# Thirteen low weight parts by ScalarE and adding transfers, and one more FFN channel by shared sums

## The chip, the core and the metric

The kernel runs on one core of a Trainium2 chip. The metric is the device time of one execution in microseconds (us). The engines are TensorE (PE in the profile; PEld is its weight load), VectorE (DVE), ScalarE (ACT), GpSimd (POOL) and SyncE (SP); sixteen DMA engines move data. Transfers are issued on SyncE's queue, and those that add to what is in the on-chip memory (SBUF) on GpSimd's.

## What is computed

One layer of a decoder trunk for 512 tokens and 1024 channels in float32, with a convolution branch and a gated linear attention branch, an output projection, and a channel mixer (FFN) of inner width F = 2816. The change lies in the up part of the FFN:

```
u2 = _rmsnorm(h, norm2_g[l])
z = _causal_dwconv(u2 @ w_ffn_up[l], ffn_dw_w[l], ffn_dw_b[l])      # 2F columns, three taps
h = h + (jax.nn.silu(z[..., :FFN_DIM]) * z[..., FFN_DIM:]) @ w_ffn_down[l]
```

## The kernel before

**Products in three.** Every float32 weight tile (128 x 1024, 512 KB) is split into a high part `whi`, rounded to the format that TensorE multiplies fast, and a low part `wlo` = tile - high. Activations are split alike (`uh`, `ul`). A product is three: low weight x high activation, high x low, high x high (`mm3`, lines 529 to 531), in this order for each of eight slices k of 128 channels.

**Splitting.** `split_weight` works through the list `order` of all weight tiles. For a plain tile, ScalarE casts `raw` to `whi` (L444) and VectorE subtracts (L452). For tiles in the set `ADDED`, all in the layer's first part until now, ScalarE writes -raw, rounded, into `wlo` (L446), and a transfer from GpSimd's queue adds the tile from DRAM to it (L447). There are four buffers each for `raw`, `whi` and `wlo`. `weight` hands a tile to the products and has the two tiles after it split (`LOOK = 2`).

**The up part.** The 2816 inner channels are 22 "channels" of 128, and each needs two tiles of `w_up`: i for the value and 22 + i for the gate. A channel is done in one of two ways:
- plain: two tiles of 24 products of 512 columns, each into one PSUM bank (`col_tile`);
- by shared sums (`two_tiles`, a "unit"): both tiles together, with seven block products in place of eight. It has four parts: x1, x3 and x2 with 24 products of 256 columns each, x4 with 12. The weight sums are made by GpSimd (`two_sums`, L386), the four subtractions for them by VectorE (L415), and the token sums of the activations once before (`ffn_sums`). ScalarE copies finished products out of PSUM (`put`, L1338), VectorE combines others (L1341). In x1 it copies the first of two products while PE makes the second; x3 then adds into the same bank.

Channels come in pairs, in three groups (`GROUPS`). After a channel's products come the convolution taps (L1717, L1720), silu (L1728) and the gating (`first_gated`, `first_of_pair` for the first of a pair, `second_of_pair` for the second). After each group its down part (`seven`, steps of `w_down`) uses the pairs.

**Order.** `up_plan` writes out, for each group, the sequence of pieces of plain tiles, parts of units and gatings. PE works in that order. The instructions of the other engines are put in order by a scheduler that has a cost for each and follows the order of the program as priority; `tc.issue_after` adds an order by hand. Before, channels 0, 2, 1, 3 and 4 in group 0 and 19 in group 2 are plain and uncut, channels 6, 7, 10, 11, 21, 14, 15 and 18 are units, and each unit has a plain channel's tiles cut into pieces between its parts: piece, x1, piece, x3, and so on.

## Time and profile before

| | |
|---|---|
| median of three runs | 819.33 us (818.31, 819.33, 819.45) |
| the profiled execution | 818.28 us |
| its span, first to last instruction | 816.5 us |
| mean granted TensorE clock | 0.998 |
| moved by DMA | 113.60 MB, mean 139 GB/s |

In the lines below, a row of the timeline has start, duration (both us), engine, source line, operation, out<-in. A row of a group has its count, busy time, mean duration in ns, and the idle time of the engine before it with what ended it. TensorE's durations overlap, since products are pipelined; the distance between starts is what one costs.

### The profile page before, as it was taken

How to read it: one execution, taken by the hardware profiler on the slowest of the kernel's cores; microseconds unless marked ns; L12 is line 12 of the kernel's file. 1: busy time of each engine (PE TensorE's matmuls, PEld its weight loads, DVE VectorE, ACT ScalarE, POOL GpSimd, SP SyncE). 2: the span in 40 equal slices, each digit the busy share in tenths (PEclk: the TensorE clock that was granted, in tenths of full speed). 3: DMA queues.
4: the chain of work that ended last, by engine and by line, in shares of the span. 5: the costliest groups of instructions: out<-in, count | busy, mean ns of one | idle time of the engine just before them, and what ended most of it. 6: DMA issues, size and time to landing. Idle time of an engine off the chain costs nothing.

```text
span 816.5 us, 11462 instructions
## 1 busy us (share of the span) xinstructions
PE 808.3 (99%) x4227; PEld 695.4 (85%) x4227; DVE 698.6 (86%) x1099; ACT 487.4 (60%) x744; POOL 197.9 (24%) x176
## 2 busy tenths in 40 slices
PE   9999999999999999999999999999999999999996
PEld 8888888788888898989888898898889988899885
DVE  6779999998998888486779899979966999789895
ACT  6667788677546575494435655556445663466554
POOL 2025434332204332122001100320123311621012
PEclk9999999999999999999999999999999999999999
DMA  8487858645831232432558513145732446335662
GB/s 329 148 195 178 196 160 179 158 114 133 192 90 65 78 130 78 136 108 93 163 132 217 184 60 123 52 154 156 147 131 83 142 117 167 104 104 180 156 129 104
DMA packets 36472, 113.60 MB, mean 139 GB/s; under 512 B 3688, under 2 KB 8944, under 8 KB 36416
## 3 DMA queue, kind: packets, MB, share of 16 engines
q1 hardware_dynamic: 28912, 86.39, 30.8%
q0 software_dynamic: 7488, 26.48, 18.7%
q8 instruction: 33, 0.54, 0.3%
q14 instruction: 23, 0.19, 0.1%
q10 hardware_dynamic: 16, 0.00, 0.0%
HBM read 110.76 MB, written 2.10 MB: 138 GB/s over the span
## 4 chain that ended last, share of the span: by engine, by line
PE 88%; DVE 11%; issue 0%; ACT 0%; POOL 0%; POOLq 0%; ACTq 0%; DVEq 0%
PE mm L529 20%; PE mm L530 20%; PE mm L531 20%; DVE c L889 5%; PE cv L529 4%; PE cv L530 4%; PE cv L531 4%; DVE aside L889 3%; PE ax L530 2%; PE ax L531 2%; PE ax L529 2%; PE mm L743 2%; PE ax L1217 1%; PE cv L743 1%; PE ax L1219 1%; PE mm L649 1%
## 5 line engine op out<-in xcount | busy, mean ns | idle before, releaser
L529 PE MATMUL mm<-uh,wlo 128*128 128x512 f32 (+1 forms) x532 | 193.9, 364 | 0.0
L530 PE MATMUL mm<-ul,whi 128*128 128x512 f32 (+1 forms) x532 | 191.5, 360 | 0.0
L531 PE MATMUL mm<-uh,whi 128*128 128x512 f32 (+1 forms) x532 | 191.4, 360 | 0.0
L415 DVE TENSOR_TENSOR wlo<-raw,whi 128x1024 fp32r<-128x1024 f32 x82 | 95.2, 1167 | 35.7 <-ACT whi L414 31.8
L386 POOL TENSOR_TENSOR raw<-raw,raw 128x512 f32<-128x512 f32 x39 | 62.7, 1609 | 234.3 <-DVE wlo L415 132.1
L529 PEld LDWEIGHTS mm<-uh,wlo 128*128 128x128 f32 x532 | 100.5, 189 | 15.3 <-DVE wlo L452 0.3
L531 PEld LDWEIGHTS mm<-uh,whi 128*128 128x128 f32 x532 | 100.4, 189 | 15.4
L530 PEld LDWEIGHTS mm<-ul,whi 128*128 128x128 f32 x532 | 100.5, 189 | 14.7
L414 ACT CAST whi<-raw 128x1024 fp32r<-128x1024 f32 x82 | 78.9, 966 | 39.3 <-PE mm L531 24.6
L444 ACT CAST whi<-raw 128x1024 fp32r<-128x1024 f32 x80 | 83.5, 1048 | 29.6 <-PE mm L531 13.9
L452 DVE TENSOR_TENSOR wlo<-raw,whi 128x1024 fp32r<-128x1024 f32 x50 | 66.2, 1329 | 7.2 <-ACT whi L444 7.0
L414 ACT CAST whi<-kept 128x1024 fp32r<-128x1024 f32 (+1 forms) x40 | 40.2, 1008 | 30.9 <-DVE kept L362 16.0
L415 DVE TENSOR_TENSOR wlo<-kept,whi 128x1024 fp32r<-128x1024 f32 (+1 forms) x40 | 47.5, 1187 | 5.8 <-ACT whi L414 5.8
L889 DVE SCALAR_TENSOR_TENSOR aside<-cv,pp,aside 128x255 f32<-128x255 f32 (+6 forms) x112 | 52.3, 467 | 0.0
L889 DVE SCALAR_TENSOR_TENSOR c<-aside,btmp,c 128x247 f32<-128x247 f32 (+13 forms) x93 | 52.2, 566 | 0.0
L889 DVE SCALAR_TENSOR_TENSOR c<-cv,pp,c 128x247 f32<-128x247 f32 (+13 forms) x93 | 43.3, 466 | 1.4 <-ACT c L885 1.4
L446 ACT ACTIVATE wlo<-raw 128x1024 fp32r<-128x1024 f32 x28 | 29.4, 1060 | 19.1 <-PE mm L529 19.1
L1338 ACT COPY tmp<-mm 128x256 f32<-128x256 f32 x38 | 14.1, 370 | 36.4 <-PE mm L531 35.8
L1720 DVE SCALAR_TENSOR_TENSOR tmp<-mm,pp,tmp 128x511 f32<-128x511 f32 (+1 forms) x42 | 31.2, 742 | 4.0 <-ACT tmp L1717 3.9
L1720 DVE SCALAR_TENSOR_TENSOR tmp<-tmp,pp,tmp 128x511 f32<-128x511 f32 (+1 forms) x32 | 27.8, 888 | 0.4
L1491 DVE TENSOR_TENSOR hres<-hres,mm 128x512 f32<-128x512 f32 (+1 forms) x37 | 24.6, 674 | 2.4 <-PE mm L531 2.0
L530 PE MATMUL cv<-ul,whi 128*128 128x512 f32 (+1 forms) x72 | 25.6, 356 | 0.0
(506 smaller groups left out, 2086.2 us busy)
## 6 DMA issues: line engine op xcount, KB each, us to landing
raw<-in_w_up_dram SPq DMA_DIRECT2D x44, 512.0 KB, 3.7
raw<-in_w_glu_dram SPq DMA_DIRECT2D x16, 512.0 KB, 5.5
raw<-in_w_down_dram SPq DMA_DIRECT2D x15, 512.0 KB, 3.9
wlo<-in_w_glu_dram POOLq DMA_DIRECT2D x12, 512.0 KB, 6.8
kept<-in_w_down_dram POOLq DMA_DIRECT2D x10, 512.0 KB, 5.8
raw<-in_w_v_dram SPq DMA_DIRECT2D x8, 512.0 KB, 6.4
raw<-in_w_qk_dram SPq DMA_DIRECT2D x8, 512.0 KB, 5.8
raw<-in_w_gb_dram SPq DMA_DIRECT2D x8, 512.0 KB, 3.9
```

The lines of the kernel that those rows point to most:

```text
L386: work = nc.gpsimd.tensor_tensor(out, x, y, ALU.add)
L414: nc.scalar.copy(hi, raw)
L415: two_low[:] = [nc.vector.tensor_tensor(lo, raw, hi.bitcast(F32), ALU.subtract)]
L444: nc.scalar.copy(hi, raw)
L446: pace[0] = nc.scalar.mul(lo, raw, -1.0)
L452: pace[0] = nc.vector.tensor_tensor(lo, raw, hi.bitcast(F32), ALU.subtract)
L529: nc.tensor.matmul(acc, ll, rh, start=first, stop=False, **kw)
L530: nc.tensor.matmul(acc, lh, rl, start=False, stop=False, **kw)
L531: nc.tensor.matmul(acc, lh, rh, start=False, stop=last, **kw)
L889: nc.vector.scalar_tensor_tensor(out[:, j:], x[:, : half_t - j], w, out[:, j:], ALU.mult, ALU.add)
L1491: done = nc.vector.tensor_tensor(hres[t, n][:, c], hres[t, n][:, c], acc[:, c], op)
L1720: nc.vector.scalar_tensor_tensor(z[:, s:], acc[:, : T - s], w[j], z[:, s:], ALU.mult, ALU.add)
```

## The change

- Channel 4 of group 0 is done by shared sums instead of plain. The plan of each group is written out in `PLANS`; the new kind "both" places the units of channels 4 and 6 around channel 5: x1 and x3 of channel 4 stand together, then tile 5 in two pieces around x2, x4, and x1 and x3 of channel 6, then tile 27 in two pieces around x2, and x4.
- An x1 that follows a gating in the plan is moved ahead of it; the value of a unit's channel is made when its gating comes and not at the end of x4.
- Thirteen plain tiles of `w_up` (1, 23, 3, 25, 8, 9, 31, 20, 35, 16, 39, 19, 41) are put in `ADDED`: ScalarE and a transfer make their low part.
- In these tiles the products go in another order (`late_low_tile`): the sixteen with the high weight part first, the eight with the low part last. Where a tile is cut, the pieces keep their number of products.

```diff
@@ -32,6 +32,8 @@
 EPS = 1e-6
 O_PAIRS = ((0, 2), (1, 3), (4, 6), (5, 7))
 GROUPS = (((0, 2), (1, 3), (4, 6), (5, 7)), ((8, 10), (9, 11), (20, 21)), ((12, 14), (13, 15), (16, 18), (17, 19)))
+PLANS = (
+(("plain",1,3),("both",4,6,5),("closes",7,8)),(("opens",10,9),("",11,20),("closes",21,12)),(("opens",14,13),("",15,16),("",18,17),("plain",19)),)
 AHEAD = 6
 
 MERGE = [("w_gb", 6, 7), ("w_ga", 0, 1), ("w_ga", 2, 3), ("w_ga", 4, 5), ("w_ga", 6, 7)]
@@ -48,6 +50,7 @@
 ADDED |= {("w_v", KT // 2 + j) for j in range(KT // 2)} | {("w_gb", m) for m in range(AHEAD)}
 POOLED = {("w_qk", 0), ("w_qk", 1)}
 ADDED -= POOLED
+ADDED |= {("w_up", j) for j in (1, 23, 3, 25, 8, 9, 31, 20, 35, 16, 39, 19, 41)}
 RATE = 5.0
 ROWS = (0, 5, 5, 5, 8, 8, 8, 8)
 EVERY = (6, 6, 6, 6, 4, 4, 4, 4)
@@ -188,48 +191,58 @@
 
     def up_plan(gi):
 
-
         pairs = GROUPS[gi]
         whole = range(KT)
 
-        def halves(*cuts):
-            return [range(a, b) for a, b in zip((0, *cuts), (*cuts, KT))]
-
-        def unit(q, f, kind):
-
-            a, b = f, FT + f
-            x1, x3, x2, x4 = (("part", q, part) for part in ("x1", "x3", "x2", "x4"))
-            a1, a2 = (("tile", a, ks) for ks in halves(4))
+        def parts(q):
+            return [("part", q, part) for part in ("x1", "x3", "x2", "x4")]
+
+        def cut(m, *at):
+            return [("tile", m, range(a, b)) for a, b in zip((0, *at), (*at, KT))]
+
+        def turns(m, role):
+            return [("tile", m, whole), ("tile", FT + m, whole), (role, m)]
+
+        def one(q, f, kind):
+
+            x1, x3, x2, x4 = parts(q)
             if kind == "opens":
-                b1, b2, b3 = (("tile", b, ks) for ks in halves(4, 6))
-                seq = [a1, x1, a2, x3, b1, x2, b2, x4, ("second", q), b3]
+                (a1, a2), (b1, b2, b3) = cut(f, 4), cut(FT + f, 4, 6)
+                seq = [a1, x1, a2, x3, b1, x2, b2, x4, role(q), b3]
             elif kind == "closes":
-                a1, a2, a3 = (("tile", a, ks) for ks in halves(3, 6))
-                seq = [x1, a1, x3, a2, x2, a3, x4, ("second", q), ("tile", b, whole)]
+                a1, a2, a3 = cut(f, 3, 6)
+                seq = [x1, a1, x3, a2, x2, a3, x4, role(q), ("tile", FT + f, whole)]
             else:
-                a1, a2 = (("tile", a, ks) for ks in halves(5))
-                b1, b2 = (("tile", b, ks) for ks in halves(4))
-                seq = [x1, a1, x3, a2, x2, b1, x4, ("second", q), b2]
-            return seq + [("first", f)]
-
-        firsts = [p for p, _ in pairs[1:]]
-        if gi + 1 < len(GROUPS):
-            firsts.append(GROUPS[gi + 1][0][0])
+                (a1, a2), (b1, b2) = cut(f, 5), cut(FT + f, 4)
+                seq = [x1, a1, x3, a2, x2, b1, x4, role(q), b2]
+            return seq + [role(f)]
+
+        def both(p, q, f):
+
+            x1, x3, x2, x4 = parts(p)
+            y1, y3, y2, y4 = parts(q)
+            (a1, a2), (b1, b2) = cut(f, 4), cut(FT + f, 4)
+            return [*(x1, x3, a1, x2, a2, x4, y1, y3, role(p), b1, y2, b2, y4, role(q)), role(f)]
+
+        seconds = {q for _, q in pairs}
+
+        def role(i):
+            return ("second" if i in seconds else "first", i)
+
         plan = []
-        n = 0
-        if gi == 0:
-            (p, q), (f, _) = pairs[1:3]
-            for i, role in ((p, "first"), (q, "second"), (f, "first")):
-                plan += [("tile", i, whole), ("tile", FT + i, whole), (role, i)]
-            n = 2
-        while n < len(firsts):
-            last = n + 1 == len(firsts) and gi + 1 < len(GROUPS)
-            kind = "closes" if last else "opens" if n == 0 else ""
-            plan += unit(pairs[n][1], firsts[n], kind)
-            n += 1
-        if n < len(pairs):
-            q = pairs[n][1]
-            plan += [("tile", q, whole), ("tile", FT + q, whole), ("second", q)]
+        for kind, *units in PLANS[gi]:
+            if kind == "plain":
+                for i in units:
+                    plan += turns(i, role(i)[0])
+            elif kind == "both":
+                plan += both(*units)
+            else:
+                plan += one(*units, kind)
+        for n in range(1, len(plan)):
+            at = n
+            while plan[n][0] == "part" and plan[n][2] == "x1" and at and plan[at - 1][0] in ("first", "second"):
+                plan[at - 1], plan[at] = plan[at], plan[at - 1]
+                at -= 1
         return plan
 
     def up_order(plan):
@@ -541,6 +554,15 @@
             if k in at:
                 at[k]()
         return acc
+
+    def late_low_tile(w, acts, acc, ks):
+
+        parts = [(w[0], k, n) for k in range(KT) for n in (0, 1)] + [(w[1], k, 0) for k in range(KT)]
+        for at in range(3 * ks.start, 3 * ks.stop):
+            x, k, n = parts[at]
+            nc.tensor.matmul(
+                acc, x[:, k * P : (k + 1) * P], acts[k][n], start=at == 0, stop=at == len(parts) - 1
+            )
 
     def row_half(name, j0, n, acts, nk, done, tok_inner, middle=None):
 
@@ -1841,7 +1863,7 @@
 
     gain3 = None
     banks, values, units = {}, {}, {}
-    third = []
+    third, found_parts = [], {}
     for gi, pairs in enumerate(GROUPS):
         acts = []
         if gi == 0:
@@ -1874,7 +1896,7 @@
                 if 0 in rest[0]:
                     banks[i] = (weight("w_up", i), mm_bank())
                 wt, acc = banks[i]
-                col_tile(wt, acts2, acc, ks=rest[0])
+                (late_low_tile if ("w_up", i) in ADDED else col_tile)(wt, acts2, acc, ks=rest[0])
                 if KT - 1 in rest[0] and i < FT:
                     values[i] = value(i, acc)
             if what == "part":
@@ -1882,13 +1904,22 @@
                     units[i] = two_tiles("w_up", i, FT + i, lambda: up_acts, ax_bank)
                 done = next(units[i])
                 if done:
-                    values[i] = value(i, done[0])
-                    banks[FT + i] = (None, done[1])
-                    third = [taps_at[0], third_ahead()]
+                    found_parts[i] = done
+                    third = [third_ahead()]
+            if what in ("first", "second") and i in found_parts:
+                done = found_parts.pop(i)
+                values[i] = value(i, done[0])
+                banks[FT + i] = (None, done[1])
+                third.append(taps_at[0])
             if what == "first":
-                w = first_gated(i, values.pop(i), banks.pop(FT + i)[1])
-                if any(i in pair for pair in pairs):
-                    found = first_of_pair(w)
+                with ExitStack() as order_of:
+                    for ins in third:
+                        if ins:
+                            order_of.enter_context(tc.issue_after(ins.ins))
+                    w = first_gated(i, values.pop(i), banks.pop(FT + i)[1])
+                    if any(i in pair for pair in pairs):
+                        found = first_of_pair(w)
+                third = []
             if what == "second":
                 with ExitStack() as order_of:
                     for ins in third:
```

## The prediction

> **What bounds the kernel now.** I read the page's busy shares first, then the same engines stage by stage over the part that the change touches, then single products on the timeline.
>
> ```profile
> span 816.5 us, 11462 instructions
> PE 808.3 (99%) x4227; PEld 695.4 (85%) x4227; DVE 698.6 (86%) x1099; ACT 487.4 (60%) x744; POOL 197.9 (24%) x176
> ```
>
> ```profile
> 492.60:514.40 21.80, 21.80 (x98) 18.03 (x97) 21.42 (x28) 10.63 (x14) 5.79 (x3) 1.00 0.26 88
> 514.40:567.30 52.90, 52.90 (x314) 47.10 (x313) 44.90 (x61) 29.82 (x44) 10.51 (x8) 1.00 0.39 122
> 567.30:605.40 38.10, 38.10 (x170) 31.55 (x169) 33.69 (x42) 17.36 (x19) 7.92 (x7) 1.00 0.59 149
> 605.40:668.40 63.00, 63.00 (x397) 57.12 (x396) 51.88 (x69) 35.44 (x53) 16.50 (x11) 1.00 0.37 115
> 668.40:697.20 28.80, 28.80 (x127) 23.48 (x126) 27.55 (x38) 12.93 (x17) 6.84 (x6) 1.00 0.58 143
> 697.20:765.70 68.50, 68.50 (x421) 61.66 (x421) 57.49 (x76) 38.98 (x57) 18.78 (x12) 1.00 0.45 146
> 765.70:816.50 50.80, 43.86 (x205) 36.61 (x203) 42.06 (x64) 26.43 (x43) 9.11 (x14) 0.96 0.47 115
> ```
>
> The second fence is the table by stretches (length, then busy time of PE, PEld, DVE, ACT, POOL, granted clock, DMA share, GB/s), cut at this kernel's stages: the first plain up tiles, the rest of group 0's up part, its down part, then the same for groups 1 and 2. PE's busy time equals the stretch in all six before the last. Busy PE is modelled, so I check it by starts: in 567.30 to 605.40 the down part has 7 x 24 = 168 products, and 38.10 / 168 is 0.227 us for each, the same as between the starts of a plain tile (5.44 / 24, next fence). Nothing in the up part waits for weights; VectorE, at 21.42 of 21.80 us in the first stretch and 27.55 of 28.80 in the fifth, is nearly full there and still not what PE waits for. So the FFN is bound by the number and size of TensorE's products, and taking work off VectorE buys room, not time. Behind PE's last product there is a tail that the change doesn't touch:
>
> ```profile
> 809.28 0.28 PE L531 MATMUL mm<-whi,ah 128*128 128x256 f32 x1
> ```
>
> From there to 816.5 the chain is additions, norm and the store.
>
> **One more channel by shared sums.** Starts on PE's timeline: a plain tile (w_up 23), then the four parts of channel 7, each from its first product to the first of what follows.
>
> ```profile
> 498.07 0.39 PE L529 MATMUL cv<-uh,wlo 128*128 128x512 f32 x1
> 503.51 0.39 PE L529 MATMUL mm<-uh,wlo 128*128 128x512 f32 x1
> 546.28 0.28 PE L529 MATMUL mm<-uh,wlo 128*128 128x256 f32 x1
> 549.15 0.40 PE L529 MATMUL mm<-uh,wlo 128*128 128x512 f32 x1
> 551.22 0.28 PE L529 MATMUL mm<-xq,wlo 128*128 128x256 f32 x1
> 554.09 0.40 PE L529 MATMUL mm<-uh,wlo 128*128 128x512 f32 x1
> 556.16 0.28 PE L529 MATMUL mm<-btmpq,wlo 128*128 128x256 f32 x1
> 559.00 0.40 PE L529 MATMUL mm<-uh,wlo 128*128 128x512 f32 x1
> 560.39 0.28 PE L529 MATMUL mm<-uh,wlo 128*128 128x256 f32 x1
> 561.83 0.40 PE L529 MATMUL cv<-uh,wlo 128*128 128x512 f32 x1
> ```
>
> A plain tile lasts 503.51 - 498.07 = 5.44 us, so channel 4 costs 10.88 us as two plain tiles (48 products of 512 columns). By shared sums x1, x3, x2 and x4 last 2.87 + 2.87 + 2.84 + 1.44 = 10.02 us (84 products of 256 columns). The saving is **0.86 us**. It is so small because a half-wide product costs 10.02 / 84 = 0.119 us and not half of 0.227: 0.012 us of each product does not shrink with its width. The number of plain pieces between half-wide ones stays the same in group 0 (both plans cut tiles 5, 27 and 8 into seven pieces), so nothing is added for changes of width.
>
> On the Trainium skill's page "TensorE: Matmul & The Clock Gate", section "Back-to-back issue gap", a product of N columns takes N/2.4 + 2.5 ns. By that the channel would go from 48 x 0.216 to 84 x 0.109 us and save an estimated 1.2 us; the starts above show a larger fixed part, and I go by them.
>
> **What that asks of the other engines.** Mean times of the groups:
>
> ```profile
> L415 DVE TENSOR_TENSOR wlo<-raw,whi 128x1024 fp32r<-128x1024 f32 x82 | 95.2, 1167 | 35.7 <-ACT whi L414 31.8
> L386 POOL TENSOR_TENSOR raw<-raw,raw 128x512 f32<-128x512 f32 x39 | 62.7, 1609 | 234.3 <-DVE wlo L415 132.1
> L444 ACT CAST whi<-raw 128x1024 fp32r<-128x1024 f32 x80 | 83.5, 1048 | 29.6 <-PE mm L531 13.9
> L452 DVE TENSOR_TENSOR wlo<-raw,whi 128x1024 fp32r<-128x1024 f32 x50 | 66.2, 1329 | 7.2 <-ACT whi L444 7.0
> L446 ACT ACTIVATE wlo<-raw 128x1024 fp32r<-128x1024 f32 x28 | 29.4, 1060 | 19.1 <-PE mm L529 19.1
> ```
>
> Channel 4 as a unit takes four subtractions (4 x 1.17) for two (2 x 1.33): 2.0 us more on VectorE, with a few short combinations some 3.5; ScalarE makes four casts instead of two and four copies out of PSUM, some 3 us; GpSimd four additions, 4 x 1.61 = 6.4 us. All of it lies beside PE's 10 us for the channel; POOL was busy for 10.51 of 52.90 us there.
>
> **Thirteen low parts by ScalarE and an adding transfer.** Each takes one subtraction (L452, 1.33 us) off VectorE, 17.3 us in all, and puts one scaled copy (L446, 1.06 us, 13.8 us in all) on ScalarE, which is busy for 29.82 of 52.90, 35.44 of 63.00 and 38.98 of 68.50 us where they fall. Off VectorE's queue this is worth nothing by itself, since PE waited for none of these subtractions. GpSimd issues thirteen transfers more, and the transfer takes its time:
>
> ```profile
> L447 POOL DMA_DIRECT2D wlo<-in_w_gb_dram x6: 847/868/924, 184.1 to 223.5; - x6
> DMA to landing us min/median/max: 5.4/7.3/11.4
> ```
>
> So issue costs POOL 13 x 0.87 = 11.3 us, and a low part that was there 1.33 us after the high one now comes 1.06 + 7.3 us after it, 12.5 us at the longest landing. That is what moving the low products to the end of the tile pays for: sixteen of a tile's 24 products need only the high part, 16 x 0.227 = 3.63 us. I worked out the room of each of the thirteen, from the end of the scaled copy to the first low product; the three tightest are w_up 9, w_up 20 and w_up 19:
>
> ```profile
> 598.77 1.05 ACT L444 CAST whi<-raw 128x1024 fp32r<-128x1024 f32 x1
> 599.86 1.75 POOL L386 TENSOR_TENSOR raw<-raw 128x512 f32<-128x512 f32 x1
> 610.97 0.40 PE L529 MATMUL cv<-uh,wlo 128*128 128x512 f32 x1
> ...
> 622.38 1.05 ACT L444 CAST whi<-raw 128x1024 fp32r<-128x1024 f32 x1 [3.75 <-PE ax L531]
> 635.56 0.40 PE L529 MATMUL mm<-uh,wlo 128*128 128x512 f32 x1
> ...
> 752.28 1.03 ACT L444 CAST whi<-raw 128x1024 fp32r<-128x1024 f32 x1
> 760.28 0.39 PE L529 MATMUL mm<-uh,wlo 128*128 128x512 f32 x1
> ```
>
> Tile 9: cast to 599.82, scaled copy to 600.88, but GpSimd is in an addition to 601.61, so the issue is then. Its second half starts at 610.97 with four high products left (0.91 us): the low part is due at 611.88, a room of 10.3 us. Tile 19: 752.28 + 1.03 + 1.06 = 754.37; due at 760.28 + 3.63 = 763.91, a room of 9.5 us. Tile 20: copied at 622.38 + 1.05 + 1.06 = 624.49; fifteen of its products precede x3, so the low part is due one product after 635.56, a room of 11.3 us. The other ten have no less than that by the same steps. At the median of 7.3 us all thirteen land in time: **0 us**. GpSimd's instruction for a transfer waits for ScalarE's copy, and queued behind it on POOL are the additions for the next unit and the down part's adding transfers; the casts of x3 and of the down part's sums wait for those. ScalarE's copy follows its cast by 1.06 us and an issue takes 0.87, so they come some 2 us later at most; POOL stood idle before them for 132.1 us waiting for VectorE (the L386 row), so I take 0.
>
> The thirteen transfers bring 6.8 MB more into stretches with a DMA share of 0.26 to 0.59, so the DMA engines have the time; a raw tile that they delay would delay its cast and count like a late low part in the first rival.
>
> The other edits: x1 of the next unit is written ahead of the work on the channel before, in groups 1 and 2 without changing PE's order; it gives the copies out of PSUM and the casts precedence over the gating, whose results are due only in the down part. 0 us.
>
> **Sum.** 0.86 us less PE work, 0 elsewhere. The profiled execution took 818.28 us, 1.8 more than its span; it would take 817.4. The median of the runs, 819.33, lies 1.05 above it, and the runs reach from 818.31 to 819.45, so I forecast 818.5 for the median: 0.10% less. A measurement of this kernel can tell about 0.2%, 1.6 us, from no change.
>
> **Rivals.** First, slower: the low parts come late. Added time is the sum over tiles of what the way from the scaled copy's end to landing has above the room: at 11.4 us for all it is 1.9 at tile 19, 1.1 at tile 9 and 0.2 at the next ones, 3.2 us, less 0.86: 820.6 by the profiled time, 821.7 by the median, 0.29% slower. It decides from about 10.3 us, where tiles 9 and 19 eat the saving. For it: each us by which ScalarE is late with the copy, or POOL with the issue, counts like one of landing, and four of the thirteen follow one another at the start of group 0. Against it: 11.4 is the longest of 28, in stretches with more traffic. On the Trainium skill's page "DMA: Bandwidth & Descriptors", section "Anatomy of one DMA", such a transfer takes 2.0 us + bytes/436e3, an estimated 3.2 us for 512 KB; the trace's shortest, 5.4, disagrees.
>
> Second: in the new unit x3 follows x1 at once, for channels 4 and 6. x3 adds into the bank from which ScalarE must first copy x1's first product, and the only cover is the second half of x1, 1.44 us. Before, a piece of a plain tile stood between. The copies out of two earlier units, PE's next product and then the copy:
>
> ```profile
> 627.82 0.28 PE L529 MATMUL ax<-uh,wlo 128*128 128x256 f32 x1
> 630.78 0.35 ACT L1338 COPY tmp<-mm 128x256 f32<-128x256 f32 x1
> ...
> 701.40 0.28 PE L529 MATMUL ax<-uh,wlo 128*128 128x256 f32 x1
> 701.60 0.37 ACT L1338 COPY tmp<-mm 128x256 f32<-128x256 f32 x1 [1.19 <-PE mm L531]
> ```
>
> It was done 3.31 us after the first product's end in the one, behind the gating, and 0.57 in the other, with nothing ahead of it. At these ends x3 waits 1.87 or 0 us, twice; I take 0, as the new order puts the copy ahead of the gating. In the middle (1.94) it is 1.0 us together: 818.4 profiled, 819.5 by the median, within 0.2%; at worst 3.7, 822.2.
>
> Third: the fixed part of a product is smaller where the new channel stands. With none, 84 half-wide products cost 42 whole ones, 6 x 0.227 = 1.36 us less: 818.0. The rule of the Trainium skill's page "TensorE: Matmul & The Clock Gate" points this way.
>
> That the change brings over 0.2% by a mechanism I don't see: PE has no idle time in the six stretches to be won, so only the 1.36 and scatter remain.
>
> **Chances.** The forecast 0.52, late low parts 0.20, late copies 0.20, the smaller fixed part 0.04, 0.04 for what I don't see. Faster by over 0.2%: a quarter of the forecast, by the scatter of 1.1 us between runs (0.13), half of the third rival and half of the unseen (0.04): 0.17. Slower: the first rival, a tenth of the second and a little of the unseen: 0.23. Within: the rest, 0.60. The range goes from 817.2 (scatter below the third rival) to 821.7 (late low parts).
>
> **What would show it.** Right: 48 PE products of 512 columns less and 84 of 256 more; PE busy for the whole of every up stretch; in group 0 the up part from the first plain tile to the first down product 0.9 us shorter; VectorE some 14 us less busy, ScalarE some 17 more; thirteen w_up transfers with landings around 7 us. Wrong: PE waiting for the transfers at the last third of tiles 9 or 19, or for a copy between x1 and x3 of channels 4 and 6; a VectorE or ScalarE order in which a cast comes after the gating, so that PE waits for a weight in a unit that had none before; or stretches shorter by over 1.4 us.

## The result, and the profile after

| | median us | lowest to highest | runs |
|---|---|---|---|
| before, beside it | 818.88 | 817.84 to 819.61 | 20 |
| after | 820.27 | 819.05 to 820.98 | 20 |

After takes 1.0016 times the time of before, 95% interval [1.0009, 1.0023]: 0.16% or some 1.3 us slower, where 0.10% less was forecast. The runs of one kernel scatter over almost 2 us, so one profiled execution can stand that far from another. After's took 820.0 us, before's 818.28.

The page's busy shares after:

```profile
span 818.3 us, 11590 instructions
PE 807.3 (99%) x4263; PEld 695.1 (85%) x4263; DVE 691.1 (84%) x1091; ACT 501.8 (61%) x763; POOL 212.1 (26%) x193
```

VectorE lost 7.5 us and not 14, ScalarE gained 14.4. The groups that answer to those shown of before:

```profile
L428 DVE TENSOR_TENSOR wlo<-raw,whi 128x1024 fp32r<-128x1024 f32 x86 | 105.0, 1227 | 36.7 <-ACT whi L427 35.2
L399 POOL TENSOR_TENSOR raw<-raw,raw 128x512 f32<-128x512 f32 x42 | 66.7, 1589 | 187.4 <-DVE wlo L428 116.1
L459 ACT ACTIVATE wlo<-raw 128x1024 fp32r<-128x1024 f32 x41 | 43.2, 1059 | 34.2 <-PE mm L542 19.0
L465 DVE TENSOR_TENSOR wlo<-raw,whi 128x1024 fp32r<-128x1024 f32 x35 | 45.2, 1299 | 5.6 <-ACT whi L457 5.4
```

Fifteen plain subtractions went (50 to 35: thirteen low parts and channel 4's two), 21.0 us. The subtractions for sums rose by four in number and by 9.8 us, since the mean of all of them rose from 1167 to 1227 ns. Where the forecast's room on VectorE is missing shows in group 0's up part, by stretches, after and then before:

```profile
487.30:514.50 27.20, 27.20 (x123) 22.51 (x121) 23.82 (x30) 18.09 (x24) 8.18 (x6) 1.00 0.53 137
514.50:567.30 52.80, 52.37 (x350) 48.14 (x349) 49.09 (x64) 34.20 (x52) 16.81 (x11) 1.00 0.44 138
```

```profile
487.20:514.40 27.20, 27.20 (x123) 22.50 (x122) 26.82 (x35) 15.92 (x20) 5.79 (x3) 1.00 0.31 98
514.40:567.30 52.90, 52.90 (x314) 47.10 (x313) 44.90 (x61) 29.82 (x44) 10.51 (x8) 1.00 0.39 122
```

VectorE's column (the third pair) sums to 72.9 us after and 71.7 before: 3.0 us of relief in the first stretch, 4.2 us more in the second, no relief in sum. The number of its instructions fell all the same, from 96 to 94 by these rows; it is their length that grew. PE, full before, is idle 0.43 us in the second stretch.

I cut every profile at TensorE's starts: first product of tile 1, first down product of group 0, end of that, and so on. The up parts of groups 1 and 2 (63.04 and 73.92 us) and the last down part (38.4) are the same in all kernels but one, and left out. The tail goes from the modelled end of the last product to the end of the span as it is printed, so it is good to 0.05 us. The lengths are those of one profiled execution of each kernel, the ratios those of all its runs. All lengths in us:

| kernel | ratio to before [95%] | up 0 | down 0 | down 1 | tail |
|---|---|---|---|---|---|
| before | | 80.13 | 38.08 | 28.84 | 6.94 |
| after | 1.0016 [1.0009, 1.0023] | 80.00 | 38.65 | 29.58 | 7.45 |
| after_again | 1.0014 [1.0004, 1.0024] | 80.19 | 38.54 | 28.71 | 7.77 |
| low_only | 1.0002 [0.9993, 1.0011] | 80.14 | 38.07 | 28.73 | 7.01 |
| ch4_only | 1.0027 [1.0018, 1.0036] | 80.98 | 39.47 | 29.05 | 7.01 |
| piece_in_4 | 1.0023 [1.0014, 1.0032] | 81.26 | 38.50 | 28.65 | 7.35 |
| no_first_four | 1.0031 [1.0020, 1.0042] | 81.20 | 38.88 | 28.70 | 7.05 |
| dve_light | 1.0024 [1.0006, 1.0043] | 79.89 | 38.53 | 29.19 | 7.57 |
| pool_light | 1.0012 [1.0001, 1.0023] | 79.32 | 38.53 | 28.93 | 7.41 |
| copy_first | 1.0012 [1.0003, 1.0021] | 79.42 | 38.52 | 28.96 | 7.83 |
| after_pad | 1.0005 [0.9996, 1.0014] | 80.02 | 38.51 | 28.65 | 7.02 |
| copy_first_pad | 0.9997 [0.9988, 1.0006] | 79.30 | 38.53 | 28.93 | 7.01 |
| copy_pad_again | 1.0001 [0.9992, 1.0010] | 79.33 | 39.55 | 28.63 | 6.97 |
| before_pad | 1.0003 [0.9995, 1.0012] | 80.13 | 38.08 | 28.66 | 6.97 |
| copy_first_30 | 1.0009 [1.0000, 1.0018] | 81.24 | 39.32 | 28.64 | 7.06 |
| copy_first_pool30 | 1.0050 [1.0036, 1.0063] | 82.57 | 38.29 | 28.64 | 6.97 |
| low_first | 1.0177 [1.0156, 1.0198] | 81.05 | 39.93 | 28.65 | 7.41 |

(low_first also has 65.52 and 82.03 us in the up parts of groups 1 and 2.) So after and after_again have up 0 where before has it, in place of 0.86 less; about 0.5 us more in down 0; and 0.4 to 0.8 us more in the tail. Down 1's 0.74 us, a wait of TensorE for an addition of VectorE's (`hres`), came in one of the two profiles only; it is put down to scatter, and no run tests its cause. I took the stages one by one.

### The profile page after: what moved, and what is told of

It reads as the page before. It is cut to its first block, busy times and chain, and to the rows that moved or that the text cites. A ratio compares the mean times of both kernels' runs of the same rounds, so it can differ in the third digit from the quotient of the medians.

```text
span 818.3 us, 11590 instructions
## 1 busy us (share of the span) xinstructions
PE 807.3 (99%) x4263; PEld 695.1 (85%) x4263; DVE 691.1 (84%) x1091; ACT 501.8 (61%) x763; POOL 212.1 (26%) x193
## 4 chain that ended last, share of the span: by engine, by line
PE 76%; DVE 18%; issue 2%; DMA 2%; ACT 1%; POOL 0%; POOLq 0%; SPq 0%; DVEq 0%; ACTq 0%
PE mm L542 15%; PE mm L543 15%; PE mm L544 15%; PE mm L563 7%; DVE c L911 5%; PE cv L542 3%; PE cv L543 3%; PE cv L544 3%; DVE aside L911 3%; DVE tmp L1742 2%; PE ax L543 2%; PE ax L544 2%; PE mm L765 2%; PE ax L542 2%; DVE wlo L428 2%
## 5 line engine op out<-in xcount | busy, mean ns | idle before, releaser
L542 PE MATMUL mm<-uh,wlo 128*128 128x512 f32 (+1 forms) x444 | 161.3, 363 | 0.0
L543 PE MATMUL mm<-ul,whi 128*128 128x512 f32 (+1 forms) x444 | 158.9, 358 | 0.0
L544 PE MATMUL mm<-uh,whi 128*128 128x512 f32 (+1 forms) x444 | 158.9, 358 | 0.0
L428 DVE TENSOR_TENSOR wlo<-raw,whi 128x1024 fp32r<-128x1024 f32 x86 | 105.0, 1227 | 36.7 <-ACT whi L427 35.2
L427 ACT CAST whi<-raw 128x1024 fp32r<-128x1024 f32 x86 | 82.6, 966 | 39.7 <-PE mm L544 26.8
L542 PEld LDWEIGHTS mm<-uh,wlo 128*128 128x128 f32 x444 | 83.9, 189 | 12.6 <-DVE wlo L465 0.3
L544 PEld LDWEIGHTS mm<-uh,whi 128*128 128x128 f32 x444 | 83.8, 189 | 12.4
L543 PEld LDWEIGHTS mm<-ul,whi 128*128 128x128 f32 x444 | 83.9, 189 | 12.0
L459 ACT ACTIVATE wlo<-raw 128x1024 fp32r<-128x1024 f32 x41 | 43.2, 1059 | 34.2 <-PE mm L542 19.0
L427 ACT CAST whi<-kept 128x1024 fp32r<-128x1024 f32 (+1 forms) x40 | 40.3, 1009 | 33.7 <-DVE kept L375 16.9
L465 DVE TENSOR_TENSOR wlo<-raw,whi 128x1024 fp32r<-128x1024 f32 x35 | 45.2, 1299 | 5.6 <-ACT whi L457 5.4
L563 PE MATMUL mm<-ul,whi 128*128 128x512 f32 x88 | 34.4, 391 | 0.0
L563 PE MATMUL mm<-uh,whi 128*128 128x512 f32 x88 | 34.3, 390 | 0.0
L1360 ACT COPY tmp<-mm 128x256 f32<-128x256 f32 x32 | 11.8, 369 | 26.9 <-PE mm L544 25.7
```

Of the source, the lines that this page charges most:

```text
L427: nc.scalar.copy(hi, raw)
L428: two_low[:] = [nc.vector.tensor_tensor(lo, raw, hi.bitcast(F32), ALU.subtract)]
L459: pace[0] = nc.scalar.mul(lo, raw, -1.0)
L465: pace[0] = nc.vector.tensor_tensor(lo, raw, hi.bitcast(F32), ALU.subtract)
L542: nc.tensor.matmul(acc, ll, rh, start=first, stop=False, **kw)
L543: nc.tensor.matmul(acc, lh, rl, start=False, stop=False, **kw)
```

## The theories

A: the copy between channel 4's x1 and x3 is late and holds TensorE for 0.70 us (the forecast's second rival). B: ScalarE or VectorE as a whole runs late through group 0. C: the thirteen transfers crowd the queues. From the first results came D (VectorE's queue sets group 0), P (GpSimd's additions slow VectorE) and E (a packet of instructions lies in the final store).

After, at the place of A: TensorE's product after x1's first, its last of x1 and the first of x3, then ScalarE, then VectorE:

```profile
515.93 0.28 PE L542 MATMUL ax<-uh,wlo 128*128 128x256 f32 x1
517.25 0.28 PE L544 MATMUL ax<-uh,whi 128*128 128x256 f32 x1
517.96 0.38 PE L542 MATMUL mm<-xq,wlo 128*128 128x256 f32 x1 [0.43 <-ACT tmp L1360]
...
515.70 1.05 ACT L1323 CAST gainq<-kept 128x1024 fp32r<-128x1024 f32 x1 [0.22 <-DVE kept L1315]
517.02 0.63 ACT L1750 ACTIVATE tmp<-tmp 128x512 f32<-128x512 f32 x1 [0.27 <-DVE tmp L1742]
517.56 0.35 ACT L1360 COPY tmp<-mm 128x256 f32<-128x256 f32 x1
...
514.45 1.21 DVE L1315 TENSOR_TENSOR kept<-kept,ul 128x1024 f32<-128x1024 f32 x1
516.19 0.74 DVE L1742 SCALAR_TENSOR_TENSOR tmp<-mm,pp,tmp 128x510 f32<-128x510 f32 x1
```

The copy could start at 515.93 and started at 517.56: ahead of it on ScalarE stand a cast for the token sums and the silu of tile 3 (L1750), and each waited for VectorE. Done at 517.91, the copy is 1.98 us late against a cover of 1.44. The start from 517.25 to 517.96 costs 0.71 in place of 0.12.

## Experiments

**The two halves of the change.** low_only puts the `ADDED` line and `late_low_tile` into the kernel before; ch4_only takes the line out of the kernel after:

```diff
-ADDED |= {("w_up", j) for j in (1, 23, 3, 25, 8, 9, 31, 20, 35, 16, 39, 19, 41)}
```

> The kernel before with the thirteen low parts and their late products alone; channel 4 stays plain. Theories for the 1.3 us by which the changed kernel is slower: (A) the copy of the first shared-sum part of channel 4 holds TensorE for 0.70 us; (B) ScalarE, crowded by the scaled copies of tiles 1, 23, 3 and 25 between 481 and 493 us, and VectorE, slowed beside GpSimd's additions for channel 4, run late through group 0, and the first tile of down group 0 waits 0.57 us; (C) the 13 adding transfers of 512 KB crowd the queues, and the casts for the down products of group 1 and the last store come 0.7 and 0.5 us later. This kernel has C's transfers and the scaled copies, and no sums in channel 4. A: the time of before (818.9) within 0.3 us. B: the time of before too, if the GpSimd additions are needed for the lateness, and up to 0.6 us over it if the scaled copies are enough. C: 1.2 us over it (820.1), with down group 1 at 29.6 us where before has 28.8.

> The changed kernel without the thirteen low parts: channel 4 by shared sums and the new order alone; VectorE subtracts those 13 low parts as before (17 us more of it than in the changed kernel). A: the copy waits for gating work that is there with and without the low parts, so the 0.70 us stay and the kernel is 0.16 us under before (818.7). B: without the scaled copies ScalarE is free at 481 to 493 us, so the copy is in time and the wait in down group 0 is smaller: 818.0 to 818.5; if on the other hand VectorE's 13 subtractions are what it lacks time for, it is slower than the changed kernel, over 820.3. C: 818.9 - 0.86 + 0.70 + 0.57 = 819.3, with down group 1 back at 28.8 us.

The low parts alone: no change, every stage as before. That refutes C by itself, for this kernel has all thirteen transfers. Channel 4 alone: 0.27% slower, more than both together. TensorE waited 1.46 us beyond the usual step for the same copy, and 0.97 us in down 0 for an addition of VectorE's (`hres`). Its first stretch:

```profile
487.90:515.10 27.20, 27.20 (x122) 22.54 (x121) 27.20 (x33) 14.97 (x20) 8.82 (x4) 1.00 0.18 59
```

VectorE is busy for 27.20 of 27.20 us. So the loss comes with the shared sums and with the order that places them, which no run takes apart, and the low parts pay part of it back by what they take off VectorE.

**Cover, or load?** piece_in_4 puts three of the eight slices of tile 5 (nine products, some 2.0 us) between x1 and x3; no_first_four leaves four low parts to VectorE.

```diff
-            (a1, a2), (b1, b2) = cut(f, 4), cut(FT + f, 4)
-            return [*(x1, x3, a1, x2, a2, x4, ...
+            (a1, a2, a3), (b1, b2) = cut(f, 3, 6), cut(FT + f, 4)
+            return [*(x1, a1, x3, a2, x2, a3, x4, ...
```

> The changed kernel with three products of tile 5 between the first and the third part of channel 4 (2.0 us more cover for the copy between them); nothing else moves but the cuts of tile 5. A: the 0.70 us at 517 us are gone, 0.7 us under the changed kernel (819.6), if the gain isn't given back in the wait for VectorE at the start of down group 0; that wait then grows by what is gained, from 0.34 to about 1.0 us, and the time stays at 820.3 (that would be B: VectorE's schedule sets group 0's end, not the copy). C: no change of the parts behind group 0.

> The changed kernel without the first four low parts (tiles 1, 23, 3 and 25; the other nine stay). VectorE gets four subtractions back (5 us), ScalarE loses four scaled copies between 481 and 493 us. A: the copy of channel 4 waits as before it, no change (820.3). B: the token sums and the gating come up to 2.9 us earlier, the copy is in time, and the wait in down group 0 is below 0.2 us: 0.7 to 1.2 us faster than the changed kernel (819.1 to 819.6). If it is VectorE's own load that is late, 5 us more of it make the wait in down group 0 longer, and the kernel is 0.3 us or more slower than the changed one. C: 4 of 13 transfers fewer, all of them landed before 500 us: down group 1 stays at 29.6 us, no change.

With the piece, the wait at 517 us is gone and one of 1.71 us beyond the usual step stands at channel 4's next copy, behind a cast that waits for VectorE:

```profile
527.11 0.38 PE L542 MATMUL ax<-gainq,wlo 128*128 128x256 f32 x1 [1.55 <-ACT tmp L1360]
...
525.96 0.83 ACT L1761 CAST sh<-v 128x768 fp32r<-128x768 f32 x1 [2.92 <-DVE v L1784]
526.69 0.37 ACT L1360 COPY tmp<-ax 128x256 f32<-128x256 f32 x1
...
522.14 1.41 DVE L1782 TENSOR_TENSOR v<-w,f 128x256 f32<-128x256 f32 x1
523.59 1.40 DVE L1783 TENSOR_TENSOR v<-v,w 128x256 f32<-128x256 f32 x1
```

(The two last take 0.42 us elsewhere.) Without the first four low parts ScalarE is freer and VectorE fuller, and the copy's wait grew to 1.80 us. So ScalarE's own load isn't the cause: VectorE is, as D has it.

**What makes VectorE late.** after_again is the kernel after, on the chip of the next three. dve_light leaves out the taps of four tiles; pool_light leaves out GpSimd's additions for channel 4 (the parts take loaded blocks in place of the sums, in lines not shown here); copy_first moves one instruction.

```diff
-        for j, s in ((1, 1), (0, 2)):
+        for j, s in () if m in (1, FT + 1, 3, FT + 3) else ((1, 1), (0, 2)):
```

```diff
         def add(out, x, y):
+            if (name, p) == ("w_up", 4): return
             work = nc.gpsimd.tensor_tensor(out, x, y, ALU.add)
```

```diff
-                    values[i] = value(i, acc)
+                    values[i] = ffn_conv(acc, i) if i == 3 else value(i, acc)
...
                 done = next(units[i])
+                if (i, rest[0]) == (4, "x1"):
+                    with tc.issue_after(puts[0].ins):
+                        nc.scalar.activation(values[3], values[3], AF.Silu)
```

> The changed kernel as it is, on the chip of the next three. All theories: 1.2 to 1.8 us over before (ratio 1.0015 to 1.0022), with a wait of about 0.7 us between the first and the third part of channel 4, some 0.3 us at the first a12 product of down group 0, and the rest (0.7 us in down group 1, 0.5 us behind the last product) only if those two are more than scatter between executions; the runs so far have down group 1 at 28.7 to 29.1 us, so I expect them gone.

> The changed kernel without the two delayed taps of the convolution in tiles 1, 23, 3 and 25 (left out of the computation: eight VectorE instructions of 0.66 us, 5.3 us of VectorE between 486 and 521 us). D (VectorE's own queue is the bound of group 0: it has no idle time there, and what stands behind it on ScalarE, the copies of channel 4's parts among it, comes late by as much as VectorE does): both waits of TensorE go, the start of down group 0 comes 0.6 to 0.8 us earlier, and the kernel is 0.8 to 1.3 us faster than the changed one, at before's time or 0.4 us under it. B' (ScalarE's own queue): its five tasks stay as they are, the copy stays late and the time stays.

> The changed kernel without GpSimd's four additions for channel 4 (its weights' sums are not formed: the parts take the loaded blocks in their place, so channels 4 and 26 come out of wrong weights; every other instruction stays). In the changed kernel three VectorE instructions beside these additions took 1.9 to 3.6 times as long as elsewhere (2.32 for 1.22 us, 1.51 for 0.42, 0.91 for 0.69 at 496 to 500 us; 1.51 for 0.67 and 1.77 for 0.68 at 521 to 524). P (it is GpSimd's access beside VectorE's that makes VectorE late): VectorE comes 2 to 4 us earlier at 505 to 524 us, the copy is in time, and the kernel is 0.7 to 1.2 us faster than the changed one. D without P (the number of VectorE's instructions alone): VectorE's times stay and so does the kernel's.

> The changed kernel with one ScalarE instruction moved: the Silu of tile 3, which waits for a VectorE tap, is issued behind the copy of channel 4's first part instead of ahead of it. A (the order on ScalarE holds TensorE): the copy ends 1.2 us after its product and not 2.0, under the 1.44 us of cover, and TensorE's wait of 0.70 us is gone; the start of down group 0 comes 0.7 us earlier. D (VectorE is the bound of the stretch): the wait goes here and comes back at the next part of channel 4 or at the start of down group 0, and the time stays within 0.3 us of the changed kernel's.

After, VectorE beside GpSimd's additions for channel 4, and the same two instructions in pool_light:

```profile
496.81 2.32 DVE L1328 TENSOR_TENSOR usq<-kept,xq 128x1024 fp32r<-128x1024 f32 x1
499.05 1.51 DVE L1782 TENSOR_TENSOR v<-w,f 128x256 f32<-128x256 f32 x1
...
495.04 3.00 POOL L399 TENSOR_TENSOR raw<-raw,raw 128x512 f32<-128x512 f32 x2
498.00 2.27 POOL L399 TENSOR_TENSOR raw<-raw 128x512 f32<-128x512 f32 x1
```

```profile
496.78 1.22 DVE L1328 TENSOR_TENSOR usq<-kept,xq 128x1024 fp32r<-128x1024 f32 x1
497.91 0.42 DVE L1782 TENSOR_TENSOR v<-w,f 128x256 f32<-128x256 f32 x1
```

With the additions gone, VectorE's token sums at 505.14 us (`usq<-kept,xq`) come at 502.91, the copy is in time, and up 0 is 79.32 us: the forecast's saving, 0.81. P holds there. It is the length of the instructions that counts: after, no idle time of ScalarE or VectorE between 480 and 530 us ends with one of GpSimd's sums. Nor is it these two alone: behind 480 us 23 of VectorE's instructions took over a quarter longer than the median of their shape (shapes with four or more), and all 23 overlapped an addition of GpSimd's. On the Trainium skill's page "SBUF — State Buffer", section "Who interferes with whom", a VectorE instruction with two SBUF inputs contends with a GpSimd instruction that reads SBUF; these rows agree: each of the two took 1.1 us more. A tap that reads PSUM and one SBUF tile kept its 0.74 us beside an addition (at 519.12 us); one of the same shape that reads two SBUF tiles took 1.77 (at 540.04).

copy_first gives nearly the same, 79.42, by order alone. Its ScalarE:

```profile
515.64 1.05 ACT L1323 CAST gainq<-kept 128x1024 fp32r<-128x1024 f32 x1 [0.22 <-DVE kept L1315]
516.60 0.36 ACT L1360 COPY tmp<-mm 128x256 f32<-128x256 f32 x1
516.97 0.63 ACT L1908 ACTIVATE tmp<-tmp 128x512 f32<-128x512 f32 x1
```

The silu is hardly later than it was (30.1 us behind the first product of tile 1, 29.8 after). A holds as the mechanism of the 0.7 us; VectorE's lateness is why the instructions ahead of the copy wait. dve_light missed: its copy is in time, but a wait of 0.45 us beyond the usual step for the next copy took half of it back, its down 0 stays, and its time is too scattered to tell.

None of the three moved down 0. In whole times the gain hardly shows: the medians of pool_light and copy_first (819.38 and 819.39) lie 0.2 us under after_again's 819.59, where P expected 0.7 to 1.2, and A the whole wait. So the 0.7 us rest on the stages, which repeat in copy_first_pad and copy_pad_again. In copy_first TensorE is done 0.39 us earlier than before's (809.17 to 809.56), yet its span is 0.5 us longer than before's: the rest is behind the last product.

**The tail.** The last store's stretch of the DMA view, after and then after_pad:

```profile
q1 hardware_dynamic: 144, 0.52, 44.1%
q14 instruction: 1, 0.01, 1.3%
issues: line engine op xcount, KB each, median us to landing
out_dram<-y SPq DMA_DIRECT2D x1, 512.0 KB, 3.0
```

```profile
q1 hardware_dynamic: 144, 0.52, 51.1%
issues: line engine op xcount, KB each, median us to landing
out_dram<-y SPq DMA_DIRECT2D x1, 512.0 KB, 2.6
```

The store's 144 packets are the same; after has a packet of the instruction queue among them, and the store lands 0.4 us later (3.4 us in copy_first). The edit of after_pad, in the FFN's set-up, changes nothing but the number of GpSimd's instructions:

```diff
+    for _ in range(16):
+        nc.gpsimd.memset(mhalf, -0.5)
```

> The changed kernel with 16 writes of a constant by GpSimd more (it writes -0.5 again over the tile that holds it), between 473 and 482 us, where GpSimd is idle; nothing waits for them. In the four profiles of the changed kernel and its near copies a packet of the instruction queue lies inside the final store, 3.7 to 4.3 us ahead of the span's end, and the store ends 2.7 to 3.0 us behind the last scaling; in the kernel before and in three others no such packet lies there and the store takes 2.25 to 2.3 us. E (the packet is GpSimd's own instructions, and it holds up one of the engines that carry the store): 16 instructions more make it come earlier than 800 us, the store takes 2.3 us again, and the kernel is 0.4 to 0.7 us faster than the changed one. If it belongs to another engine, or the store is late for another reason, it stays at 2.7 us or more and the time stays.

> Both at once: the Silu of tile 3 behind the copy, and GpSimd's 16 writes. If the copy's 0.70 us and the store's 0.4 to 0.7 us are the two things by which the changed kernel is over before, TensorE ends some 0.4 us ahead of before's 809.56 and the store as long as there: 0.3 to 0.5 us under before, ratio 0.9994 to 0.9996. If the packet isn't GpSimd's: as the kernel with the Silu moved, ratio 1.0012.

> The kernel before with the 16 GpSimd writes. E (they only move the place at which GpSimd's instructions are fetched): before has no packet inside the store, so nothing is gained; ratio 1.000 within 0.0005, and up to 1.0010 if the move puts a packet into the store here. If the writes speed the kernel up by themselves: 0.6 us or more under before, as in the changed kernel with them.

> The changed kernel with both repairs again (the Silu of tile 3 behind the copy, the 16 writes). If the 0.9997 of the first set holds: 0.9990 to 1.0004. By its stages: up group 0 79.4 us (before 80.1), down group 0 38.5 (38.1), the rest as before: 0.3 us under before.

The packet is gone from the store, the tail is 7.0 us again, and the kernel is at 1.0005 (its interval overlaps that of after_again): E holds, with 0.4 to 0.8 us of tail. before_pad shows that the writes do nothing by themselves. The packet that before has at 809.7 us stayed with 16 writes more (810.3, in an execution whose FFN began 0.85 us later), which speaks against its being GpSimd's. Both repairs together, twice: 0.9997 and 1.0001, no difference from before that can be measured.

E does not cover every long tail. In pool_light, piece_in_4 and low_first the store takes the usual 2.6 us and the tail is 7.4 us all the same: the span ends 2.0 to 2.1 us behind the landing, where it is 1.6 to 1.7 in the others, and what comes late there is GpSimd's closing instructions. No run tests the cause.

On the Trainium skill's page "Runtime: NRT & Kernel Launch", section "Instruction fetch mechanics", an engine fetches its instructions by DMA in blocks, and crossing a block is "mostly hidden". Here the one that lies inside the last transfer is not hidden; what the others of that queue (23 to 25 in all) cost was not measured.

**What is left in down 0.** VectorE in the changed kernel, the low part for the second a12 product; then before:

```profile
578.15 0.39 PE L542 MATMUL ax<-whi,al 128*128 128x512 f32 x1
578.62 0.50 PE L543 MATMUL ax<-wlo,ah 128*128 128x512 f32 x1
...
577.34 1.22 DVE L428 TENSOR_TENSOR wlo<-raw,whi 128x1024 fp32r<-128x1024 f32 x1
```

```profile
578.17 0.39 PE L529 MATMUL ax<-whi,al 128*128 128x512 f32 x1
578.40 0.39 PE L530 MATMUL ax<-wlo,ah 128*128 128x512 f32 x1
...
575.61 1.22 DVE L415 TENSOR_TENSOR wlo<-raw,whi 128x1024 fp32r<-128x1024 f32 x1
```

VectorE is 1.7 us later with it, at the end of thirty microseconds in which it has no idle time. But that stretch holds no more work than before's, it begins later. Its beginning, after (ScalarE, then VectorE) and then before:

```profile
544.94 0.62 ACT L1761 CAST yh<-w 128x512 fp32r<-128x512 f32 x1 [1.87 <-DVE w L1772]
546.42 1.04 ACT L427 CAST whi<-raw 128x1024 fp32r<-128x1024 f32 x1
...
547.49 2.44 DVE L428 TENSOR_TENSOR wlo<-raw,whi 128x1024 fp32r<-128x1024 f32 x2 [1.20 <-ACT whi L427]
```

```profile
544.00 1.05 ACT L414 CAST whi<-raw 128x1024 fp32r<-128x1024 f32 x1
...
545.09 1.23 DVE L415 TENSOR_TENSOR wlo<-raw,whi 128x1024 fp32r<-128x1024 f32 x1 [2.28 <-ACT whi L414]
```

From this subtraction to the low part in question it is 29.85 us after (547.49 to 577.34) and 30.52 before (545.09 to 575.61). What is late is ScalarE's cast of a weight (L427). It stands behind a cast of channel 4's gating (L1761), which waits for VectorE, whose two taps ahead of it took 1.77 and 1.68 us beside GpSimd's additions; before, channel 4's gating was cast at 531.59 us, long out of the way. As far as these rows go, the wait comes from where the new plan puts that gating, which the forecast priced at nothing; no run moves it.

Two kernels take 1.2 us of VectorE out of that stretch, with tile 30's low part made by ScalarE and a transfer, or by GpSimd:

```diff
-ADDED |= {("w_up", j) for j in (1, 23, 3, 25, 8, 9, 31, 20, 35, 16, 39, 19, 41)}
+ADDED |= {("w_up", j) for j in (1, 23, 3, 25, 8, 9, 31, 20, 35, 16, 39, 19, 41, 30)}
```

```diff
-POOLED = {("w_qk", 0), ("w_qk", 1)}
+POOLED = {("w_qk", 0), ("w_qk", 1), ("w_up", FT + 8)}
```

> The same with the low part of tile 30 by ScalarE and an adding transfer too: VectorE loses 1.2 us in the stretch from 546 to 586 us, in which it has no idle time in the changed kernel and its last result before TensorE's wait (the low part at 577 us for the first a12 product of down group 0's second block) comes 1.7 us later than in before. D: that wait (0.34 us) goes, 0.3 us under the kernel without it. Against it: tile 30's block is cast at 556 us and its low products begin some 8.5 us later, while adding transfers of this size took 6.9 us in the middle behind 2.4 us of scaled copy and issue; if it lands late, TensorE waits up to 1 us at 565 us, and the kernel is slower by that.

> The same with the low part of tile 30 formed by GpSimd (two subtractions of 128x512, by its additions here 1.3 us each alone and up to 2.3 beside VectorE) and its products last in the tile, where 3.6 us more are to be had; VectorE loses its subtraction of 1.22 us at 557 us. D: down group 0 comes to 38.1 or 38.2 us, 0.3 to 0.4 us under copy_pad_again. If GpSimd's subtractions slow VectorE by as much as they take from it (1.1 us at 496 us in the changed kernel): no change, or up to 0.5 us over it.

Both were slower than copy_first_pad. In the one, the low part landed late and TensorE waited 1.13 us for it, and later for `hres`, as in ch4_only. In the other GpSimd's two subtractions slowed VectorE by 2.3 us where they saved it 1.2, and TensorE waited 2.92 us for a combination of VectorE's (L1363). Only some 1.1 of these can be the slowing: VectorE's order changed too, and has three instructions ahead of that combination (L1774, L1764 twice) that follow it in copy_first_pad. The rows of the slowing:

```profile
557.54 2.75 POOL L463 TENSOR_TENSOR wlo<-raw,whi 128x512 fp32r<-128x512 f32 x2 [6.68 <-DVE v L1785]
557.55 1.57 DVE L1786 TENSOR_TENSOR v<-f,v 128x256 f32<-128x256 f32 x1
559.04 1.79 DVE L1758 TENSOR_TENSOR w<-tmp,tmp 128x512 f32<-128x512 f32 x1
```

The wait for the second a12 product is gone in both, which proves little, since TensorE came to it 1.9 and 3.3 us later. That VectorE's lateness makes the 0.45 us is read from the rows and not shown by a run. One more thing in down 0 comes and goes: copy_pad_again has 39.55 there and copy_first_pad, the same kernel, 38.53. The adding transfers into `kept` at 584 us took, in copy_first_pad and then copy_pad_again:

```profile
DMA to landing us min/median/max: 7.5/8.7/9.8
```

```profile
DMA to landing us min/median/max: 9.9/11.1/12.3
```

At 12.3 us the second of the casts behind them starts at 597.58 us and not at 595.72, `hres` is late, and TensorE waits 0.94 us. Before issues these two at 582.37 and 584.10, after at 584.22 and 585.84, behind VectorE's subtractions.

**The late low products.** low_first has `col_tile` for all tiles.

```diff
-                (late_low_tile if ("w_up", i) in ADDED else col_tile)(wt, acts2, acc, ks=rest[0])
+                col_tile(wt, acts2, acc, ks=rest[0])
```

> The changed kernel with the products in the old order in the thirteen tiles too: high and low parts alternate, so a low part is needed with the tile's first three products and not after two thirds of it (7.3 us earlier). If the late place of the low products is what hides the transfers (6.9 us in the middle): TensorE waits in several of the thirteen tiles, 2 to 30 us in all, and the kernel is slower by that. If the low parts land early in any case: within 0.3 us of the changed kernel.

14.5 us slower than before, as the first of the two expectations had it. TensorE waits at five tiles for the transfer itself, 9.9 us of the 11.8 by which its profiled execution is longer than after's; three of them:

```profile
608.10 0.50 PE L542 MATMUL mm<-uh,wlo 128*128 128x512 f32 x1 [1.35 <-DMA wlo<-in_w_up_dram]
634.35 0.50 PE L542 MATMUL mm<-uh,wlo 128*128 128x512 f32 x1 [2.07 <-DMA wlo<-in_w_up_dram]
717.23 0.50 PE L542 MATMUL mm<-uh,wlo 128*128 128x512 f32 x1 [3.59 <-DMA wlo<-in_w_up_dram]
```

## Why the prediction was wrong

The forecast was a saving of 0.86 us and zero for all else. By its own steps:

- **One more channel by shared sums**: right. Where no copy waits (copy_first, copy_first_pad, copy_pad_again, pool_light) up 0 is 0.71 to 0.83 us shorter. The third rival, a smaller fixed part of a product, did not show. The rule of N/2.4 + 2.5 ns that the prediction sets beside its sum stands on the Trainium skill's page "TensorE: Matmul & The Clock Gate", section "Back-to-back issue gap", for a single product by itself; the 1.2 us worked out from it were not seen.
- **Thirteen low parts**: right, with the reason. They landed after

```profile
DMA to landing us min/median/max: 5.0/6.9/10.6
```

and TensorE waited for none; alone they change nothing, and low_first shows that the order of the products is what hides them.
- **"I take 0, as the new order puts the copy ahead of the gating"**: this step failed. It was the second rival, and its middle (1.94 us after the product) was what happened at channel 4 (1.98); that the mean of two rows came so near is luck. It cost 0.69 us (0.59, and 0.10 at the next product) of the 0.86. The copy does stand ahead of channel 3's gating, but behind the silu of channel 3's value and a cast for the token sums. The forecast looked for one thing ahead of the copy and not for the others, though one of its two rows had the copy 3.31 us late. Channel 6's copy was in time.
- **"All of it lies beside PE's 10 us"** and **"VectorE some 14 us less"**: failed. The 14 us was a sum over the FFN; 7.5 came, most of them in the up parts of groups 1 and 2 (1.6 and 5.7). In group 0's up part VectorE had 71.7 of 80.1 us. With the low parts alone it had 68.1 (low_only), with channel 4's own instructions 70.1 (pool_light), with GpSimd's additions beside them 72.9 (after): these additions, priced at nothing for VectorE, took back what was left of the relief and 1.2 us more. The rows that the prediction quoted said 21.42 of 21.80; they were read as an engine nearly full that nothing waits for, without asking what a microsecond more would push out. "Wrong" named a cast behind the gating, and that is what the rows show at 545 us, though what waited was the down part. The cost is 0.45 us in down 0, read from rows, and 1 us more in one execution (copy_pad_again).
- **GpSimd's additions, "beside PE"**: mis-sized by what they do to VectorE: 1.1 us on each of the two instructions shown, 2.8 us over group 0's up part by pool_light.
- **"A tail that the change doesn't touch"**: failed, 0.4 to 0.8 us, for a reason that no row of the prediction could show.

In sum, for after_again, up 0, down 0 and tail: 0.06 + 0.46 + 0.83 = 1.35 us, less 0.13 in down 1: 1.2 us, 0.15%, beside the measured 0.14%. That it comes so near is partly luck: stages are of one execution each, and the spans of these two differ by 1.5 us, of which 0.27 came ahead of the FFN. The 0.7 us of the copy and the store's delay were each taken away by a run; the 0.45 us were not. No version run here beats before.

## What to carry to other kernels

An engine that is full in a stretch is priced by that stretch and by what is queued behind it, not by its sum over the kernel, and what an idle neighbour is given counts there too if it lengthens the full engine's instructions: work added there comes out as a wait elsewhere, and more cover at one place moves the wait to the next. For a copy that frees a PSUM bank, list every instruction that the copying engine has ahead of it, with what each waits for; one instruction moved was worth 0.7 us here. When a small change moves the tail, look for instruction packets in the last store before explaining it by the change.

## What the hardware did that was not expected

- One packet of the instruction queue inside the last store (512 KB, 2.6 us) made it land at 3.0 to 3.4 us; sixteen short instructions on GpSimd, over 300 us earlier, took it away.
- Two of VectorE's instructions with both inputs in SBUF took 2.32 for 1.22 us, and 1.51 for 0.42, beside GpSimd's additions; GpSimd's took up to 2.27 for 1.3.
- The same two adding transfers of the same kernel landed after at most 9.8 us in one execution and 12.3 in another.
